# Seven large expert positions, outputs combined in quarters, and f32 one-hot picks in a two-layer mixture-of-experts kernel

## The chip, the cores and the metric

The kernel runs on one core of a Trainium2 chip, in one launch. The metric is the device time of one execution in microseconds, as the median of several. All times below are microseconds, and times of day in the trace count from the start of the span.

## The reference, cut to what matters

Two layers of a backbone. Each mixes tokens (attention and retention heads, an output projection) and then sends every token through two of 16 experts. Layer 0 does this for 512 tokens (256 latent, 256 context), layer 1 for the 256 latent ones. The expert part is:

```python
s = sigmoid(h @ w_router)
grouped = (s + b_router).reshape(-1, 4, 4)
grp = argmax(top_k(grouped, 2)[0].sum(-1))
e_idx = grp * 4 + top_k(grouped[grp], 2)[1]
gate = s[e_idx] / sum(s[e_idx])
a, u = split(x_e @ w_gu[e], 2)
y_e = (silu(a) * u) @ w_down[e]
x = x + g2 * sum_over_two_experts(gate * y_e)
```

Here h is the normalized and modulated x, w_gu[e] is 1024 x 2048, w_down[e] is 1024 x 1024, all f32, and g2 is one row of 1024 for the latent and one for the context tokens. The result must hold to f32 accuracy, so matmuls that go at full speed run on values split in a high and a low part, three products for one.

## The kernel before, in words

**Weights.** Each expert's 12 MB come as 12 pages of 1 MB (eight gate/up pages, four down pages, tile w) through one queue, SP's, into a ring of pages that x, gathered rows, outputs and constants share. The order of the stream is gate/up of expert 0, down of 0, gate/up of 1, gate/up of 2, down of 1 and so on; the last is down of expert 15. A page's transfer is issued when an earlier page has been given back.

**Positions.** The experts of a layer are run in an order that the kernel finds by counting tokens. BIG_AT names the positions that take a large expert: nine of 16 in layer 0, three in layer 1. A large position holds up to 128 rows in layer 0 (96 in layer 1): ScalarE makes the high part of each page (L190), VectorE the low part (L192), and TensorE runs three products of 128 x 512 for each logical one (L200, L201, L202; gu and dn). A small position holds up to 64 rows and multiplies the page as it is, in f32, with the rows as the stationary operand (gs at L1301, ds at L1317). The table rho says which rank by count goes to which position; position 0 is always expert 0. If an expert has more tokens than its position holds, a branch at L1387 is entered that runs every expert again in a loop, 128 rows at a time.

**Rows.** In layer 0 the rows of h are written to DRAM (HX) and an indirect DMA gathers those of an expert, which TensorE then transposes (fl, L1282). In layer 1 they stay in SBUF, in three bf16 parts (x3, L1024 to L1030), and a small expert's rows are picked by 48 one-hot bf16 matmuls (L1244; two tiles of 128 tokens, eight column blocks, three parts); for a large one by place (L1227). Index and gate of each slot come from one-hot matmuls as well (idx L1178, gates L1189, four matmuls each in layer 0).

**Routing** (route) is a chain of small VectorE steps: counts, ranks, the order, then `arranged` puts positions and gates into the order of the run; after it comes the branch. Out_proj's rows() makes h: in layer 0 two tiles on VectorE and two on ScalarE and GpSimd (L1012).

**Outputs.** An expert's rows are scattered into Y in DRAM with accumulation (L1367). After expert 13, combine reads Y back (four transfers yy in layer 0, two in layer 1, issued by GpSimd, L1535), multiplies it by g2 (L1537) and adds it to x (L1538), on VectorE. The last two experts don't go through DRAM: finish takes the down product of expert 15 in four quarters of 256 columns (L1589), spreads the rows of 14 and 15 to the tokens with one-hot matmuls (fin, L1565), multiplies by g2 (ftmp, L1575) and adds to x (L1577), where GpSimd makes one of the two adds of layer 0. A small expert's hidden rows are the product of silu(a) and u (L1306 on ScalarE, L1307 on VectorE) and are turned by TensorE (tu, L1273) ahead of its down product.

The tile framework orders the instructions of each engine when the program is built; every engine then runs them in that order.

Of the kernel before, what the change touches and what calls it, by code (L numbers as in the profile page):

```python
# [9 lines left out]
F32 = mybir.dt.float32  # L10
# [21 lines left out]
BIG_AT = [(0, 2, 4, 5, 7, 8, 10, 11, 13), (0, 4, 8)]  # L32
# [28 lines left out]
class Kernel:  # L61
# [199 lines left out]
    def late_consts(self):  # L261
# [60 lines left out]
        for l, runs in enumerate((((0, 1, 1, 15), (2, 4, 3, 0), (4, 4, 3, 4), (3, 4, 3, 8), (1, 1, 1, 12), (14, 2, 1, 13)),  # L322
                                  ((0, 1, 1, 15), (4, 2, 4, 0), (1, 3, 1, 2), (5, 3, 1, 5), (9, 7, 1, 8)))):
            for r in runs:
                i_(l, *r)
# [4 lines left out]
        self.tok = cp.tile([128, 4, 2], BF, name="tok")  # L330
        g.iota(self.tok[:, :, 0], pattern=[[128, 4]], base=-BIG, channel_multiplier=0, allow_small_or_imprecise_dtypes=True)
        g.iota(self.tok[:, :, 1], pattern=[[0, 4]], base=0, channel_multiplier=1, allow_small_or_imprecise_dtypes=True)
        self.tok2 = cp.tile([128, 4, 2], BF, name="tok2")
        v.tensor_scalar(self.tok2, self.tok, 2.0, None, op0=OP.mult)
# [568 lines left out]
    def out_proj(self, l):  # L903
# [103 lines left out]
        def rows():  # L1007
            for t in range(nt):
                b = mb[:, (t // 2) * 1024:(t // 2) * 1024 + 1024]
                if t % 2 and not l:  # L1010
                    nc.scalar.activation(xr[t], xr[t], AF.Copy, scale=rs[:, t:t + 1])
                    nc.gpsimd.tensor_tensor(xr[t], xr[t], b, op=OP.add)  # L1012
                else:
                    v.scalar_tensor_tensor(xr[t], xr[t], rs[:, t:t + 1], b, op0=OP.mult, op1=OP.add)
                nc.sync.dma_start(self.HX[l][t * 128:(t + 1) * 128, :], xr[t])
            if l:

                self.hx = [self.pgs.get("hx") for _ in range(2)]
                x3 = self.x3 = [self.hx[i // 2][1][:, (i % 2) * 1024:(i % 2) * 1024 + 1024].bitcast(BF).rearrange("p (t n) -> p t n", t=2)
                                for i in range(3)]  # L1020
                for t in range(nt):
                    nc.scalar.activation(x3[0][:, t], xr[t], AF.Copy)
                for t, rest in enumerate((ma, mb)):
                    nc.gpsimd.tensor_tensor(rest, xr[t], x3[0][:, t], op=OP.subtract)  # L1024
                    nc.scalar.activation(x3[1][:, t], rest, AF.Copy)

        def parts():
            if l:
                for t, rest in enumerate((ma, mb)):
                    v.tensor_tensor(self.x3[2][:, t], rest, self.x3[1][:, t], op=OP.subtract)  # L1030
            for i, _ in mg + xg:
                self.pgs.put(i)

        self.parts = parts

        return lg, rows


    def route(self, l, lg, rows):
# [10 lines left out]
        t1, t2 = (room[:, 320 + i * 16:320 + i * 16 + n4] for i in range(2))  # L1050
        nc.scalar.activation(s, lg[:, :nt], AF.Exp, scale=-1.0)
        warm = self.tiny("warm", [128, 1])
        nc.scalar.activation(warm, s[:, 0, 0:1], AF.Silu)
        rows()
# [24 lines left out]
        ve = g4[:, :, :, None].to_broadcast(o)  # L1079
        vo = g4[:, :, None, :].to_broadcast(o)  # L1080
        v.tensor_tensor(c1, vo, ve, op=OP.is_gt)
        v.tensor_tensor(c2, vo, ve, op=OP.is_equal)
# [15 lines left out]
        for t in range(nt):  # L1098
            nc.tensor.matmul(cnt, ones, sel[:, t], start=t == 0, stop=t == nt - 1)
        posm = self.tiny("rpm", [128, nt, 16], bufs=1)  # L1100
# [8 lines left out]
        self.indices(l, 0)  # L1109

# [6 lines left out]
        perm = sq()  # L1117
        v.tensor_tensor(perm, rank[:, None, :].to_broadcast(b16), self.rho[:, l, :, None].to_broadcast(b16), op=OP.is_equal)
        v.tensor_tensor(c3, perm, self.eid[:, None, :].to_broadcast(b16), op=OP.mult)
        od = self.tiny("rod", [128, 16], bufs=1)  # L1120
        v.tensor_reduce(od, c3, axis=AX.X, op=OP.add)
        order = self.cp.tile([128, 16], I32, name=f"order{l}")
        v.tensor_copy(order, od)

        def arranged(dst, src, e=v):
            for t in range(nt):
                m = self.sm.tile([128, 512], F32, tag="P", name="sq", bufs=3)[:, 0:256].rearrange("p (a b) -> p a b", b=16)
                e.tensor_tensor(m, perm, src[:, t, None, :].to_broadcast(b16), op=OP.mult)
                v.tensor_reduce(dst[:, t], m, axis=AX.X, op=OP.add)

        self.posm = self.tiny("rpr", [128, nt, 16], bufs=1)
        arranged(self.posm, posm)
        self.order[l] = order

# [15 lines left out]
        ve = self.ve = self.tiny("rve", [128, nt, 16, 3], BF, bufs=1)  # L1150
# [5 lines left out]
        with self.tc.issue_after(self.placed.ins):  # L1156
            self.parts()
        g = nc.gpsimd
        g.tensor_tensor(kx, s, gd[:, :, None].to_broadcast([128, nt, 16]), op=OP.mult)
        arranged(kw, kx, g)  # L1160
        for c in range(3):
            g.tensor_copy(ve[:, :, :, c], kw)
            if c < 2:
                g.tensor_tensor(kw, kw, ve[:, :, :, c], op=OP.subtract)

    def index(self, posm, S, idx, tok=None, room=None, folded=False):

        nc = self.nc
        nt = posm.shape[1]
        if room is None:  # L1170
            room = self.sm.tile([128, 512], BF, tag="oh", name="oh", bufs=2)
# [4 lines left out]
        p = self.bank("B", "idx")[:S]  # L1176
        for t in range(nt):
# [3 lines left out]
        self.placed = nc.vector.tensor_scalar(idx, p[:, 0:1], p[:, 1:2], self.halfc[:S] if folded else float(BIG), op0=OP.add, op1=OP.add)  # L1181
        return oh

    def gates(self, oh, ve, gate):

        nt, S = oh.shape[1:]
        p = self.bank("B", "gates")[:S]
        for t in range(nt):
            self.nc.tensor.matmul(p[:, 0:3], oh[:, t], ve[:, t], start=t == 0, stop=t == nt - 1)  # L1189
        self.nc.vector.tensor_reduce(gate, p[:, 0:3], axis=AX.X, op=OP.add)  # L1190

    def indices(self, l, e):
        S = self.slots(l, e)
        self.oh[e % 2] = self.index(self.posm[:, :, e], S, self.idx[:S, e:e + 1],
# [24 lines left out]
    def place(self, p, oh, b, parts=range(3)):  # L1219

        nt, S = oh.shape[1:]
        for i in parts:
            x = self.x3[i]
            for t in range(nt):
                for f in range(4):
                    c = (b * 4 + f) * 128
                    self.nc.tensor.matmul(p[:, f * S:(f + 1) * S], x[:, t, c:c + 128], oh[:, t],  # L1227
                                          start=i == t == f == 0, stop=i == 2 and t == nt - 1 and f == 3)

    def pick_up(self, l, e, b):  # L1230

        nc = self.nc
        if not self.big(l, e):
# [7 lines left out]
            for i in range(3):  # L1241
                for t in range(nt):
# [9 lines left out]
        else:  # L1252
            p = self.early[b]
            self.place(p, self.oh[0], b, (2,))
# [116 lines left out]
    def overflow(self, l):  # L1371
# [15 lines left out]
        with tc.If(n > 0):  # L1387
            for base in range(0, T - SMALL, 128):
                with tc.For_i(0, NE, 1) as e:
                    pe = self.tiny("ope", [128, nt], bufs=1)  # L1390
                    vv = self.tiny("ovv", [128, nt, 3], BF, bufs=1)
# [3 lines left out]
                    for c in range(3):  # L1395
                        nc.vector.tensor_copy(vv[:, :, c], kx)
                        nc.vector.tensor_tensor(kx, kx, vv[:, :, c], op=OP.subtract)
# [3 lines left out]
                    self.gates(self.index(pe, 128, ix, room=oh), vv, og)  # L1401
# [31 lines left out]
    def moe(self, l):  # L1433
# [24 lines left out]
        if last:  # L1458
            self.early = [self.bank("CB"[b], "pl") for b in range(2)]
            for b in range(2):  # L1460
                self.place(self.early[b], self.oh[0], b, (0, 1))
            self.overflow(l)
            room()
            pg.extend(self.hx)
            for b in range(2):
                self.pick_up(l, 0, b)
        else:
            room()
            pg.append(self.pgs.get("ex"))
            self.xg = [pg[1][1][:, b * 1024:(b + 1) * 1024] for b in range(2)]  # L1470
            nc.gpsimd.memset(pg[1][1], 0.0)
            self.expert_load(l, 0)
            self.overflow(l)
# [9 lines left out]
        def between(e):  # L1483

            def f(k):
# [5 lines left out]
                if k == 2:  # L1491
# [31 lines left out]
    def combine(self, l):  # L1523
# [12 lines left out]
        for t in range(nt):  # L1536
# [172 lines left out]
```

## Time and profile before

| | |
|---|---|
| three runs | 1628.0, 1632.47, 1633.39 (median 1632.47) |
| profiled execution | 1638.47, of which the span 1636.4 |
| TensorE, VectorE, ScalarE, GpSimd busy in the span | 1448.4, 874.8, 615.5, 161.1 |
| mean granted clock of TensorE | 0.961 of 2.4 GHz |
| moved by DMA | 515.64 MB, mean 315 GB/s |
| experts of layer 0, first gate/up product to the last add to x | 362 to 924 |
| experts of layer 1, the same | 1144 to 1633 |

A row of the trace gives its start, its length, engine, line, operation and tiles with shapes, how many alike stood together, and in brackets how long the engine had waited before it and for what. Matmul rows overlap, so a group's length is read from first to last.

### The profile page before, as it was taken

What the parts mean: (1) busy time and instruction counts of PE and PEld (TensorE: products, weight loads), DVE (VectorE), ACT (ScalarE), POOL (GpSimd) and SP (SyncE); (2) the same over time, 40 slices, a digit from 0 to 9 for tenths busy, and PEclk for the clock granted to TensorE, in tenths of its full rate; (3) what the DMA queues carried; (4) which work ended last, traced back from release to release, by engine and by line L of the source; (5) the groups of instructions that cost most, each with busy time, mean ns of one, the idle gap of its engine ahead of it and who ended that gap; (6) DMA issues with size and microseconds to landing.
All of it is one profiled execution on the core that took longest, in us unless ns stands there. A gap on an engine that the chain in (4) does not pass through costs nothing. (4 is left out here: it accounts for less than half of the span.)

```text
span 1636.4 us, 21740 instructions
## 1 busy us (share of the span) xinstructions
PE 1448.4 (89%) x7858; PEld 870.9 (53%) x7858; DVE 874.8 (53%) x1658; ACT 615.5 (38%) x922; POOL 161.1 (10%) x208
## 2 busy tenths in 40 slices
PE   5999999929999999999994799983999999988876
PEld 4767756716666567565741577762545435422213
DVE  5776576476666577575732586877525305300003
ACT  3353404225556456464630454542424304300000
POOL 2000000440010000100000400012000000000000
PEclk9999999959999999999997899996999999999998
DMA  9763679528999999999796744561899999999996
GB/s 268 288 224 132 258 267 351 180 108 340 409 405 413 391 392 353 387 390 371 292 356 262 270 134 150 189 262 40 332 419 415 418 412 419 419 414 418 417 415 225
DMA packets 115674, 515.64 MB, mean 315 GB/s; under 512 B 14145, under 2 KB 40417, under 8 KB 61922
## 3 DMA queue, kind: packets, MB, share of 16 engines
q1 hardware_dynamic: 102176, 488.67, 76.1%
q0 software_dynamic: 8016, 17.42, 3.8%
q10 hardware_dynamic: 5362, 8.03, 1.5%
q8 instruction: 65, 1.06, 0.3%
q14 instruction: 55, 0.45, 0.1%
HBM read 503.24 MB, written 17.48 MB: 318 GB/s over the span
## 5 line engine op out<-in xcount | busy, mean ns | idle before, releaser
L192 DVE TENSOR_TENSOR lo<-w,hi 128x1024 fp32r<-128x1024 f32 x342 | 417.2, 1231 | 108.8 <-ACT hi L190 36.1
L190 ACT ACTIVATE hi<-w 128x1024 fp32r<-128x1024 f32 x344 | 359.2, 1059 | 169.4 <-PE gu L202 48.4
L1301 PE MATMUL gs<-w,ex 128*64 128x512 f32 x1280 | 296.1, 600 | 24.8 <-DMA w<-in_w_gate_up_dram 24.5
L1301 PEld LDWEIGHTS gs<-w,ex 128*64 128x64 f32 x1280 | 83.2, 136 | 193.8 <-issue 130.4
L201 PE MATMUL gu<-lo,ex 128*128 128x512 f32 (+1 forms) x384 | 152.4, 397 | 0.5 <-DVE lo L192 0.5
L202 PE MATMUL gu<-hi,ex 128*128 128x512 f32 (+1 forms) x384 | 151.4, 395 | 0.0
L1317 PE MATMUL ds<-w,ex 128*64 128x512 f32 x576 | 139.7, 618 | 3.1 <-DMA w<-in_w_down_dram 3.0
L200 PE MATMUL gu<-hi,ex 128*128 128x512 f32 (+1 forms) x384 | 133.8, 405 | 7.9 <-ACT hi L190 7.7
L200 PE MATMUL px<-hi,hT 128*128 128x512 f32 (+1 forms) x304 | 114.7, 382 | 0.6 <-ACT hm L507 0.6
L201 PE MATMUL px<-lo,hT 128*128 128x512 f32 (+1 forms) x304 | 114.8, 378 | 0.0
L202 PE MATMUL px<-hi,hT 128*128 128x512 f32 (+1 forms) x304 | 114.2, 376 | 0.0
L1307 DVE TENSOR_TENSOR ex<-ex,gs 128x512 f32<-128x512 f32 x20 | 13.7, 687 | 178.9 <-PE gs L1301 178.9
L1367 POOL DMA_INDIRECT y<-ex,ridx x28 | 43.6, 1558 | 603.5 <-ACT ex L1323 357.3
L1306 ACT ACTIVATE ex<-gs 128x512 f32<-128x512 f32 x20 | 11.9, 597 | 235.0 <-PE gs L1301 235.0
L200 PEld LDWEIGHTS gu<-hi,ex 128*128 128x128 f32 (+1 forms) x384 | 70.0, 185 | 30.5 <-ACT hi L190 13.8
L201 PEld LDWEIGHTS gu<-lo,ex 128*128 128x128 f32 (+1 forms) x384 | 70.5, 184 | 22.8 <-DVE lo L192 3.9
L201 PE MATMUL dn<-lo,ex 128*128 128x512 f32 (+1 forms) x192 | 80.2, 418 | 2.1 <-DVE lo L192 1.8
L202 PEld LDWEIGHTS gu<-hi,ex 128*128 128x128 f32 (+1 forms) x384 | 70.3, 183 | 16.8
L202 PE MATMUL dn<-hi,ex 128*128 128x512 f32 (+1 forms) x192 | 77.2, 402 | 0.0
L1317 PEld LDWEIGHTS ds<-w,ex 128*64 128x64 f32 x576 | 37.6, 140 | 73.6 <-issue 56.9
L200 PE MATMUL dn<-hi,ex 128*128 128x512 f32 (+1 forms) x192 | 67.9, 411 | 1.7 <-ACT hi L190 1.6
L200 PEld LDWEIGHTS px<-hi,hT 128*128 128x128 f32 x304 | 57.0, 189 | 20.2 <-issue 5.2
(348 smaller groups left out, 1900.7 us busy)
## 6 DMA issues: line engine op xcount, KB each, us to landing
w<-in_w_gate_up_dram SPq DMA_DIRECT2D x256, 1024.0 KB, 12.0
w<-in_w_down_dram SPq DMA_DIRECT2D x128, 1024.0 KB, 11.4
w<-in_ada_w_dram SPq DMA_DIRECT2D x40, 1024.0 KB, 6.7
w<-in_w_in_dram SPq DMA_DIRECT2D x20, 1024.0 KB, 7.8
w<-in_ada_w_dram SPq DMA_DIRECT2D x16, 512.0 KB, 8.6
w<-in_w_out_dram SPq DMA_DIRECT2D x8, 1024.0 KB, 6.7
y<-zero POOLq DMA_DIRECT2D x3, 1024.0 KB, 10.7
g<-modd ACTq DMA_DIRECT2D x6, 512.0 KB, 6.3
```

What stands on the lines that cost most here:

```text
L190: nc.scalar.activation(hi, w, AF.Copy)
L192: (nc.gpsimd if after else nc.vector).tensor_tensor(lo, w, hi.bitcast(F32), op=OP.subtract)
L200: mm(o, a[0], b[0], start=first, stop=False)
L201: mm(o, a[0], b[1], start=False, stop=False)
L202: mm(o, a[1], b[0], start=False, stop=last)
L1301: nc.tensor.matmul(ps[n // 2][(n % 2) * 64:(n % 2) * 64 + 64], x[:, self.part(k)], t[:, n * 512:(n + 1) * 512], start=k == 0, stop=k == 7)
L1306: nc.scalar.activation(h, ps[0], AF.Silu)
L1307: nc.vector.tensor_tensor(h, h, ps[1], op=OP.mult)
L1317: nc.tensor.matmul(p[n * 64:n * 64 + 64], self.sx[2][:, self.part(ff)], t[:, f * 1024 + n * 512:f * 1024 + n * 512 + 512], start=ff == 0, ...
L1367: self.nc.gpsimd.indirect_dma_start(out=dst, out_offset=bass.IndirectOffsetOnAxis(ap=idx, axis=0), in_=y, in_offset=None, bounds_check=n - ...
```

## The change

1. BIG_AT of layer 0 names seven positions (0, 2, 4, 6, 8, 10, 12) where it named nine; rho follows. Positions 13, 14 and 15 are small. Layer 1 keeps its three.
2. combine only issues the reads of Y. finish does the rest by quarters: it adds Y's columns to what the one-hot matmuls gave (L1577), multiplies by g2 (L1578) and adds to x (L1580), all on VectorE. The pages of Y are kept until finish ends.
3. Layer 1 keeps x's rows in f32, without the three parts, and picks them with 16 f32 one-hot matmuls (L1257, place L1241) for the 48 in bf16.
4. Routing: out_proj hands out single rows(t), all on VectorE; the branch comes ahead of `arranged`, which goes to VectorE whole; in layer 1 the first expert's picks stand ahead of the branch; gather and its memset of layer 0's first expert come earlier.
5. Index and gate come out of one matmul per tile (L1190): the gate's columns stand beside the index's. Only expert 0's gates are still made apart (L1204).

```diff
-BIG_AT = [(0, 2, 4, 5, 7, 8, 10, 11, 13), (0, 4, 8)]
+BIG_AT = [(0, 2, 4, 6, 8, 10, 12), (0, 4, 8)]
...
+        def row(t):
+            b = mb[:, (t // 2) * 1024:(t // 2) * 1024 + 1024]
+            v.scalar_tensor_tensor(xr[t], xr[t], rs[:, t:t + 1], b, op0=OP.mult, op1=OP.add)
+            nc.sync.dma_start(self.HX[l][t * 128:(t + 1) * 128, :], xr[t])
...
+        v.tensor_tensor(kx, kw, gd[:, :, None].to_broadcast([128, nt, 16]), op=OP.mult)
+        if l:
+            self.early = [self.bank("CB"[b], "pl") for b in range(2)]
+            for b in range(2):
+                self.place(self.early[b], self.oh[0], b)
+        self.overflow(l)
+        perm = sq()
...
+        arranged(self.posm, self.posm)
+        if parts == 1:
+            arranged(ve[:, :, :, 2], kx)
...
-            nc.tensor.matmul(p[:, 0:2], oh[:, t], (self.tok2 if folded else self.tok)[:, t], start=t == 0, stop=t == nt - 1)
+            nc.tensor.matmul(p[:, 0:n], oh[:, t], ve[:, t, 0:n], start=t == 0, stop=t == nt - 1)
...
-            for i in range(3):
-                for t in range(nt):
-                    for k in range(8):
-                        nc.tensor.matmul(p[:, self.part(k)], self.x3[i][:, t, k * 128:(k + 1) * 128], oh[:, t, 0:64],
-                                         start=i == t == k == 0, stop=i == 2 and t == nt - 1 and k == 7)
+            for t in range(nt):
+                for k in range(8):
+                    nc.tensor.matmul(p[:, self.part(k)], self.xr[t][:, k * 128:(k + 1) * 128], oh[:, t, 0:64],
+                                     start=t == k == 0, stop=t == nt - 1 and k == 7)
...
-        for t in range(nt):
-            nc.vector.tensor_tensor(y[t], y[t], g2[:, (t // 2) * 1024:(t // 2) * 1024 + 1024], op=OP.mult)
-            nc.vector.tensor_tensor(self.x[t], self.x[t], y[t], op=OP.add)
-        for i, _ in yg:
-            self.pgs.put(i)
+        self.yg = yg
...
-                nc.vector.tensor_tensor(tmp, two(acc[r]), g[:, None].to_broadcast([128, 2, 256]), op=OP.mult)
-                x = two(self.xpg[r][1])[:, :, j * 256:j * 256 + 256]
-                add = (nc.gpsimd if r == 0 and pairs == 2 else nc.vector).tensor_tensor(x, x, tmp, op=OP.add)
+                nc.vector.tensor_tensor(tmp, two(acc[r]), two(self.yg[r][1])[:, :, c], op=OP.add)
+                nc.vector.tensor_tensor(tmp, tmp, g[:, None].to_broadcast([128, 2, 256]), op=OP.mult)
+                x = two(self.xpg[r][1])[:, :, c]
+                add = nc.vector.tensor_tensor(x, x, tmp, op=OP.add)
```

The order of instructions on VectorE at the end of layer 0, before (yy is what was read of Y, ex at L1307 the last small expert's hidden rows):

```order
L192 TENSOR_TENSOR lo<-w,hi 128x1024 x6
L1537 TENSOR_TENSOR yy<-yy,g_7712 128x1024
L1538 TENSOR_TENSOR xs<-xs,yy 128x1024
L1537 TENSOR_TENSOR yy<-yy,g_7712 128x1024 x2
L1538 TENSOR_TENSOR xs<-xs,yy 128x1024 x2
L1537 TENSOR_TENSOR yy<-yy,g_7712 128x1024
L1538 TENSOR_TENSOR xs<-xs,yy 128x1024
L1307 TENSOR_TENSOR ex<-ex,gs 128x512
L97 COPY ex<-tu 128x512
```

And with the change, where L1319 is what L1307 was:

```order
L192 TENSOR_TENSOR lo<-w,hi 128x1024 x8
L1319 TENSOR_TENSOR ex<-ex,gs 128x512 x2
L97 COPY ex<-tu 128x512
L1610 SCALAR_TENSOR_TENSOR ex<-ds,rgate,ex 128x512
L1610 SCALAR_TENSOR_TENSOR ex<-dn,rgate,ex 128x256
L1577 TENSOR_TENSOR ftmp<-fin,yy 128x512
L1610 SCALAR_TENSOR_TENSOR ex<-dn,rgate,ex 128x256
L1578 TENSOR_TENSOR ftmp<-ftmp,g_7190 128x512
```

The eight steps on yy no longer stand ahead of the last small expert's hidden rows; yy is first read in finish.

On TensorE at layer 1's branch (over is the number that the branch tests), with the change:

```order
L1096 MATMUL pos<-rsel,ones 128x16
L1190 MATMUL idx<-rve,oh 96x2 x2
L1241 MATMUL pl<-oh,xr 128x96 x16
L1388 TENSOR_LOAD over_9366
L1399 COMPARE_AND_BRANCH
L1401 COMPARE_AND_BRANCH
```

All 16 f32 picks of the first expert now stand ahead of the branch, where 48 in bf16 (L1227) stood before.

## Rows read from the trace of the kernel before

**Rows 1.** Stretches of 20 us: busy time (instructions), granted clock, DMA share, GB/s.
```profile
800.00:820.00 20.00, 20.00 (x94) 13.83 (x94) 13.87 (x14) 11.13 (x12) 0.00 (x0) 1.00 0.56 210
...
880.00:900.00 20.00, 7.89 (x28) 2.94 (x30) 8.79 (x8) 0.00 (x0) 0.00 (x0) 0.57 0.39 149
...
1120.00:1140.00 20.00, 4.36 (x55) 3.91 (x55) 17.16 (x55) 4.31 (x6) 7.93 (x11) 0.59 0.13 49
```

**Rows 2.** Two stretches, TensorE alone: busy (instructions), clock, DMA share, GB/s.
```profile
417.20:477.60 60.40, 60.40 (x296) 1.00 1.02 409
514.20:618.50 104.30, 98.26 (x449) 0.98 1.01 393
```

**Rows 3.** DMA of a stretch, packets and rate: 410 to 912.
```profile
DMA packets 32611, 184.70 MB, mean 368 GB/s; under 512 B 4780, under 2 KB 8868, under 8 KB 11912
```

**Rows 4.** The same of 400 to 540.
```profile
DMA packets 8684, 57.35 MB, mean 410 GB/s; under 512 B 1262, under 2 KB 1262, under 8 KB 2004
```

**Rows 5.** The same of 1180 to 1600.
```profile
DMA packets 25869, 175.03 MB, mean 417 GB/s; under 512 B 3768, under 2 KB 3768, under 8 KB 4947
```

**Rows 6.** Timeline of TensorE in layer 0: two products, then the tail.
```profile
368.40 0.39 PE L200 MATMUL gu<-hi,ex 128*128 128x512 f32 x1
368.62 0.39 PE L201 MATMUL gu<-lo,ex 128*128 128x512 f32 x1
...
872.12 1.94 PE L1301 MATMUL gs<-w,ex 128*64 128x512 f32 x8 [0.54 <-DMA w<-in_w_gate_up_dram]
892.11 1.12 PE L1273 MATMUL tu<-ident,ex 128*128 128x128 f32 x4 [18.05 <-DVE ex L1307]
...
904.19 1.95 PE L1589 MATMUL dn<-w,ex 128*64 128x256 f32 x16
...
907.88 1.95 PE L1589 MATMUL dn<-w,ex 128*64 128x256 f32 x16
```

**Rows 7.** Timeline of VectorE in the same tail.
```profile
878.62 1.23 DVE L1537 TENSOR_TENSOR yy<-yy,g 128x1024 f32<-128x1024 f32 x1 [22.92 <-DMA yy<-y]
...
891.38 0.68 DVE L1307 TENSOR_TENSOR ex<-ex,gs 128x512 f32<-128x512 f32 x1
...
910.18 0.69 DVE L1575 TENSOR_TENSOR ftmp<-fin,g 128x512 f32<-128x512 f32 x1 [3.00 <-PE fin L1565]
...
922.52 1.05 DVE L1577 TENSOR_TENSOR xs<-xs,ftmp 128x512 f32<-128x512 f32 x1
```

**Rows 8.** Waits of TensorE in layer 1, 1143 to 1632: total, times, longest.
```profile
PE gs L1301 <- DMA w<-in_w_gate_up_dram: 20.7, 29, 1.8
...
PE ds L1317 <- DMA w<-in_w_down_dram: 3.0, 6, 0.6
```

**Rows 9.** TensorE: bf16 picks of one small expert, and 32 f32 instructions of another matmul.
```profile
1208.82 1.57 PE L1244 MATMUL pl<-oh,hx 128*128 128x64 bf16 x48
...
1065.28 3.74 PE L810 MATMUL ro<-rv,am 128*128 128x128 f32 x32
```

**Rows 10.** Weight loads of that f32 matmul: min, median, max in ns.
```profile
L810 PEld LDWEIGHTS ro<-rv,am x160: 186/192/192, 206.9 to 1068.6; 128*128 128x128 f32 x160
```

**Rows 11.** Routing of layer 1 on GpSimd, VectorE and TensorE, in the timeline.
```profile
1120.51 4.20 POOL L1024 TENSOR_TENSOR mods<-xr,hx 128x1024 f32<-128x1024 f32 x2 [7.80 <-issue]
...
1117.57 2.48 DVE L1014 SCALAR_TENSOR_TENSOR xr<-xr,n2r,mods 128x1024 f32<-128x1024 f32 x2
...
1120.56 2.12 DVE L1057 TENSOR_TENSOR room<-room,brt 128x32 f32<-128x32 f32 x1
...
1142.20 0.29 PE L1189 MATMUL gates<-rve,oh 128*96 128x3 bf16 x2 [7.11 <-PEq L1387]
```

**Rows 12.** Routing of layer 0 on VectorE and GpSimd.
```profile
333.77 4.56 DVE L1014 SCALAR_TENSOR_TENSOR xr<-xr,n2r,mods 128x1024 f32<-128x1024 f32 x2
...
334.47 6.06 POOL L1012 TENSOR_TENSOR xr<-xr,mods 128x1024 f32<-128x1024 f32 x2 [1.96 <-ACT xr L1011]
```

**Rows 13.** Tail of layer 1 on TensorE.
```profile
1604.52 1.11 PE L1273 MATMUL tu<-ident,ex 128*128 128x128 f32 x4 [3.80 <-DVE ex L1307]
```

More of the change, by code (lines that the diff above doesn't have):

```diff
@@ L321, in late_consts @@
                                              allow_small_or_imprecise_dtypes=True)
[L322 removed]
+        for l, runs in enumerate((((0, 1, 1, 15), (2, 6, 2, 0), (1, 7, 2, 6), (14, 2, 1, 13)),
                                   ((0, 1, 1, 15), (4, 2, 4, 0), (1, 3, 1, 2), (5, 3, 1, 5), (9, 7, 1, 8)))):
@@ L1005, in out_proj, with route @@
             v.scalar_tensor_tensor(lg[:, t], lg[:, t], rs[:, t:t + 1], self.c0[l][:, t // 2], op0=OP.mult, op1=OP.add)
-        def rows():
-            for t in range(nt):
[L1009 to L1020, printed above, removed]
-                for t in range(nt):
[L1022 to L1025, printed above, removed]
+        def row(t):
+            b = mb[:, (t // 2) * 1024:(t // 2) * 1024 + 1024]
+            v.scalar_tensor_tensor(xr[t], xr[t], rs[:, t:t + 1], b, op0=OP.mult, op1=OP.add)
+            nc.sync.dma_start(self.HX[l][t * 128:(t + 1) * 128, :], xr[t])
         def parts():
[L1028 to L1031, printed above, removed]
+            for i, _ in mg + xg * (1 - l):
                 self.pgs.put(i)
+        self.rows, self.xr = xg, xr
         self.parts = parts
-        return lg, rows
-    def route(self, l, lg, rows):
+        return lg, row
+    def route(self, l, lg, row):
         nc = self.nc
@@ L1050, in route @@
         t1, t2 = (room[:, 320 + i * 16:320 + i * 16 + n4] for i in range(2))
+        if l == 0:
+            self.xgp = self.pgs.get("ex")
+            nc.gpsimd.memset(self.xgp[1], 0.0)
         nc.scalar.activation(s, lg[:, :nt], AF.Exp, scale=-1.0)
         warm = self.tiny("warm", [128, 1])
-        nc.scalar.activation(warm, s[:, 0, 0:1], AF.Silu)
-        rows()
+        nc.scalar.activation(warm, lg[:, 0, 0:1], AF.Silu)
+        parts = 1 if l == DEPTH - 1 else 3
+        ve = self.ve = self.tiny("rve", [128, nt, 16, 2 + parts], F32 if parts == 1 else BF, bufs=1)
+        for c in range(2):
+            nc.gpsimd.tensor_tensor(ve[:, :, :, c], self.tok[:, 0:nt, c, None].to_broadcast([128, nt, 16]),
+                                    self.rowsof[:, l, None, :].to_broadcast([128, nt, 16]), op=OP.mult)
+        row(0)
         v.tensor_scalar(s, s, 1.0, None, op0=OP.add)
@@ L1099, in route @@
             nc.tensor.matmul(cnt, ones, sel[:, t], start=t == 0, stop=t == nt - 1)
+        for t in range(1, 3 if l == 0 else 2):
+            row(t)
         posm = self.tiny("rpm", [128, nt, 16], bufs=1)
@@ L1109, in route @@
         self.indices(l, 0)
+        if l == 0:
+            row(3)
+            self.xg = [self.xgp[1][:, b * 1024:(b + 1) * 1024] for b in range(2)]
+            self.expert_load(l, 0)
         b16 = [128, 16, 16]
@@ L1116, in route @@
         v.tensor_reduce(rank, c3, axis=AX.X, op=OP.add)
[L1117 to L1133, printed above, removed]
         self.posx = posm
@@ L1155, in route, with arranged, index @@
         v.reciprocal(gd, gd)
[L1156 to L1166, printed above, removed]
+        v.tensor_tensor(kx, kw, gd[:, :, None].to_broadcast([128, nt, 16]), op=OP.mult)
[5 more added lines that the diff above has]
+        perm = sq()
+        v.tensor_tensor(perm, rank[:, None, :].to_broadcast(b16), self.rho[:, l, :, None].to_broadcast(b16), op=OP.is_equal)
+        v.tensor_tensor(c3, perm, self.eid[:, None, :].to_broadcast(b16), op=OP.mult)
+        od = self.tiny("rod", [128, 16], bufs=1)
+        v.tensor_reduce(od, c3, axis=AX.X, op=OP.add)
+        order = self.cp.tile([128, 16], I32, name=f"order{l}")
+        v.tensor_copy(order, od)
+        self.order[l] = order
+        def arranged(dst, src):
+            m = self.hip.tile([128, 1024], F32, tag="hl", name="pm", bufs=5)[:, 0:nt * 256].rearrange("p (t a b) -> p t a b", a=16, b=16)
+            o = [128, nt, 16, 16]
+            v.tensor_tensor(m, perm[:, None].to_broadcast(o), src[:, :, None, :].to_broadcast(o), op=OP.mult)
+            v.tensor_reduce(dst, m, axis=AX.X, op=OP.add)
+        self.posm = self.tiny("rpr", [128, nt, 16], bufs=1)
+        v.tensor_tensor(self.posm, posm, cap[:, None, :].to_broadcast([128, nt, 16]), op=OP.add)
+        arranged(self.posm, self.posm)
+        if parts == 1:
+            arranged(ve[:, :, :, 2], kx)
+        else:
+            arranged(kw, kx)
+            for c in range(3):
+                v.tensor_copy(ve[:, :, :, 2 + c], kw)
+                if c < 2:
+                    v.tensor_tensor(kw, kw, ve[:, :, :, 2 + c], op=OP.subtract)
+        self.parts()
+    def index(self, posm, S, idx, ve, gate=None, tok=None, room=None, folded=False):
         nc = self.nc
@@ L1217, in expert_load, with place @@
             self.gather(l, self.xg[e % 2][:, 0:512], self.idx[:, e:e + 1], True)
-    def place(self, p, oh, b, parts=range(3)):
+    def place(self, p, oh, b):
         nt, S = oh.shape[1:]
[L1222 to L1228, printed above, removed]
+        for t in range(nt):
+            for f in range(4):
+                c = (b * 4 + f) * 128
+                self.nc.tensor.matmul(p[:, f * S:(f + 1) * S], self.xr[t][:, c:c + 128], oh[:, t],
+                                      start=t == f == 0, stop=t == nt - 1 and f == 3)
     def pick_up(self, l, e, b):
@@ L1458, in moe @@
         if last:
[L1459 to L1462, printed above, removed]
             room()
-            pg.extend(self.hx)
+            pg.extend(self.rows)
             for b in range(2):
@@ L1468, in moe @@
             room()
[L1469 to L1473, printed above, removed]
+            pg.append(self.xgp)
             for b in range(2):
@@ L1490, in f @@
                         self.turn(self.h, self.sx[2], True)
-                if k == 2:
+                if k == 2 and not e:
                     self.gates(self.oh[e % 2], self.ve[:, :, e], self.gate[:self.slots(l, e), e:e + 1])
@@ L1598, in finish @@
         rest(*done)
-        for i in (self.g2[0], ti):
+        for i in (self.g2[0], ti, *(i for i, _ in self.yg)):
             self.pgs.put(i)
@@ L1672, in run @@
         K.mixers(l)
-        lg, rows = K.out_proj(l)
-        K.route(l, lg, rows)
+        lg, row = K.out_proj(l)
+        K.route(l, lg, row)
         K.moe(l)
```

47 lines of the change are left out of this document (27 added, 20 removed).

## The prediction

> **What bounds the kernel now.** I read the stretches of 20 us first, because the two layers have different limits. In layer 0's experts (362 to 924) the share of the DMA is high but not whole: it drops to 0.56 at 800 to 820 and to 0.39 at 880 to 900, and in the second of these TensorE is busy for 7.89 of 20 us at a granted clock of 0.57, so mostly at the lower of its two levels, 1.2 GHz [rows 1]. In the first TensorE is busy throughout, so pages were not given back fast enough; the second is a stall. Then two longer stretches, which compare the mix of positions: where one large and one small expert alternate they take 60.4 together, and where two large stand beside one small, the three take 104.3 and TensorE is no longer gapless [rows 2]. Then the rate of the transfers: layer 0 averages 368 GB/s from 410 to 912 [rows 3], had 410 in its early, alternating part [rows 4], and layer 1 runs at 417 for 420 us on end [rows 5]. So layer 1 is bound by its weights, and layer 0 by its engines, somewhat below the stream. Last the timeline of the tail: TensorE finishes the last small expert's gate/up at 874, then waits 18.05 for VectorE's product of its hidden rows [rows 6]. That product itself takes 0.68; VectorE could not begin it before 891.38, because the eight steps on the outputs read back from DRAM stand ahead of it, and the first of them waited 22.92 for its data [rows 7].
>
> **The change, part by part.** All durations are of the profiled execution, 1638.47 with a span of 1636.4; it stands 6.0 above the median of the runs, so I subtract from it and then take off the same 6.0.
>
> *Two large positions become small.* A large expert has 96 + 48 products 0.22 to 0.23 apart, 33 us of TensorE; a small one has 12 pages of eight instructions at 1.94, 23.3 [rows 6]. That is 9.5 saved per position, 19 for two: the low end, as it counts TensorE alone. From the stretches, a further large expert costs 104.3 - 60.4 = 43.9, so a small one 16.5, and two exchanges would give 55 [rows 2]: the high end, since it also counts the waits for splits where two large ones follow each other, which no longer happens. TensorE was still busy 98.26 of the 104.3, so the value lies near the low end: **-22**. ScalarE's and VectorE's splits of 24 pages go as well; neither bounds the new pattern, which the gapless stretch of 417 to 477 shows.
>
> *The stall in the tail.* The order shown with the change has the hidden rows' product directly behind the splits. Of 18.05 only the product's own 0.7 stays: **-17**. The wait for Y does not vanish by itself. Its reader is now the first step of finish, which stood at 910.18 [rows 7], 31.6 after the first transfer was there; the read hangs on expert 13's scatter and moves up with it. I cost it at nothing. If that cover goes, it is up to 12, what lay between the first step's start and the hidden rows' product.
>
> *The ceiling of these two.* From 410 to 912 the DMA moved 184.70 MB [rows 3]. At 410 GB/s that takes 450.5, so the stream would end at 860, 51 earlier; at 417, 59 earlier; at the 393 of the stretch with two large ones, 470, 32 earlier. The new pattern is that of the stretch with 409, so 39 fits under the ceiling, with some 12 to spare.
>
> *Index and gate in one matmul.* Fifteen groups like the 0.29 one of two matmuls [rows 11] go; at most 4 in layer 0, partly beside waits: **-2**. In layer 1 it lies under the DMA: 0.
>
> *Finish of layer 0.* Each quarter had three steps on VectorE and one on GpSimd, and now has six on VectorE of 0.69 each, 4.1 where TensorE takes 907.88 - 904.19 = 3.7 per quarter [rows 6, 7]. VectorE so becomes the bound by 0.4 each, and behind the last quarter stand all six steps instead of about three: **+4** (0 to +6). The two pages of Y are held until then; the next weights wanted are the projection's of layer 1, 13 us behind the last add, so 0.
>
> *Routing of layer 0.* Before, two tiles of rows took VectorE 4.56, because GpSimd's 6.06 ran beside them [rows 12]. Four tiles on VectorE alone cost 5.0, if two take the 2.48 which they take in layer 1 [rows 11]. `arranged`, now behind the branch, leaves the path to the branch and joins the path behind it. Taken as 0, between -3 and +5.
>
> *Routing of layer 1.* GpSimd's 4.20 of subtraction goes, beside which two tiny VectorE steps took some 2 us each, the first 2.12 [rows 11]; `arranged` goes behind the branch. Against this, 16 f32 picks stand ahead of it: 3.74 at the full clock [rows 9], up to 7.5 at half of it; 0.59 was granted there, so mostly the lower level [rows 1]. The experts start **-5** earlier (-8 to +1), and the first page of weights as well.
>
> *f32 picks in layer 1.* Forty-eight bf16 matmuls took 1.57. The trace has no f32 pick; the nearest row is a f32 matmul with the same 128 x 128 stationary operand, of which 32 instructions (two for each of 16 products) took 3.74 [rows 9]. So +2.2 per expert, and 13 small ones and two large, +32 on TensorE. The other end: if the loads, 0.192 each [rows 10], don't overlap, 6.1 per expert and +68. I take the first, since that row already holds such loads. The cover is 23.7 of TensorE's waits for weights in this layer [rows 8]; **+8** are left, and if there were none, +32. The rule that speaks against this step is in the Trainium skill, FP8 and Floating Point Precision, TensorE Precision Notes: true f32 goes through the array in four passes. Three bf16 products would so become four passes, an estimate of 2.1 instead of 3.74, and layer 1 would keep the whole of its earlier start. The row is the dearer of the two, and I go by the row.
>
> *Tail of layer 1.* The same wait, 3.80 [rows 13], becomes 0.7, and one step of 0.69 is added behind the last quarter: **-2**.
>
> Sum: layer 0 -22 - 17 - 2 + 4 = -37; layer 1 -5 + 8 - 2 = +1; together -36. From 1638.47 this is 1602.5, and less 6.0, **1596**.
>
> **The rivals.** *The stream can't go faster (0.20).* The DMA's share stood at 1.01 at 393 GB/s too [rows 2]; if this means that it was full, only its holes can be filled: 0.44 of 20 and 0.61 of 20 [rows 1], 21. Then -21 + 4 + 1 = -16: 1616. Against it stands that the same mix of weights and gathers ran at 410 earlier [rows 4]. *The whole ceiling (0.12).* The exchange is worth what the stretches say, the stream ends 51 earlier, and layer 1 keeps its early start of 5: -51 + 4 - 5 = -52: 1580. *f32 picks at their loads' pace (0.05).* +68 less 24 of cover, less 5 and 2, is +37 and eats the whole gain: 1633, no change. *The branch is taken (0.03).* This one ends slower. With seven large positions the eighth largest count of layer 0, not counting expert 0, must fit 64 rows; counted from the inputs by the reference it is exactly 64. One token more, by a near tie decided the other way in the kernel's arithmetic, and the loop runs 16 experts four times, 12 MB each: 805 MB, at 410 GB/s [rows 4] 1964, so about 3560. From the 65th token on it decides; below, it costs nothing. For it speaks only that there is no slack.
>
> **How the numbers follow.** The forecast has 0.60. Range 1576 to 1620: it holds the forecast with the bounds of its terms, the whole ceiling, and most of the case in which only the holes are filled. A measurement of this kernel can tell about 0.3% (5 us) from no change. Faster by more: the forecast and the first two rivals, 0.92, less 0.01 for bounds that fall together. Within: 0.05. Slower: 0.04.
>
> **What would show it.** Right: no wait above 1 at the hidden rows' turn in either tail; layer 0's last add near 887 in place of 922.52 [rows 7]; 400 GB/s or more from 410 to the end of layer 0's weights; a pick of 16 products near 3.7; TensorE's waits for weights in layer 1 near nothing while its end comes as much earlier as layer 0's. The forecast is wrong if the rate in layer 0 stays under 380 without a hole, if the first step of finish waits for Y, or if layer 1's experts take over 10 more than the 489 from 1144 to 1633.

## The result, and the profile after

The changed kernel takes 1613.39 as a median of four runs (1607.81 to 1615.39), the one before 1632.93: a ratio of 0.988, 95% interval 0.9846 to 0.9913, or 19.5 less. 1596 was forecast, in a range of 1576 to 1620. The profiled execution took 1607.81, the fastest of the four, at a granted clock of 0.968, where the profiled one of before, 1638.47, stood above its median, at 0.961; so the two traces differ by 30.7, more than the medians do. I use the traces to see where time went, and medians to price it.

The page of the changed kernel, the span and the busy times:

```profile
span 1606.0 us, 20671 instructions
...
PE 1451.1 (90%) x7434; PEld 872.1 (54%) x7434; DVE 799.9 (50%) x1604; ACT 562.4 (35%) x864; POOL 139.5 (9%) x195
```

TensorE is busy as long as before, in a span that is 30 shorter: what the exchange took off in layer 0 (498 to 469 between the first gate/up product and expert 15's down product), the f32 picks added in layer 1 (438 to 471 over its experts).

Stretches of layer 0, TensorE alone (us, busy, granted clock, DMA share, GB/s), to be held against [rows 2]:

```profile
416.60:537.90 121.30, 119.46 (x557) 1.00 1.02 409
537.90:664.90 127.00, 121.15 (x545) 0.99 1.02 412
664.90:799.80 134.90, 123.18 (x539) 0.97 0.96 381
799.80:865.00 65.20, 48.75 (x210) 0.97 1.01 395
```

Each of the first three is two pairs of a large and a small expert. They take 121, 127 and 135: the 60.4 per pair of [rows 2] holds at first, then the stream sets the pace at 410 GB/s, and then it falls to 381; why it falls is not shown. DMA of 405 to 870, against [rows 3]:

```profile
DMA packets 32147, 185.73 MB, mean 399 GB/s; under 512 B 4564, under 2 KB 8336, under 8 KB 11199
```

The tail of layer 0 on TensorE, against [rows 6]:

```profile
848.02 1.94 PE L1313 MATMUL gs<-w,ex 128*64 128x512 f32 x8 [1.83 <-DMA w<-in_w_gate_up_dram]
850.82 0.66 PE L1285 MATMUL tu<-ident,ex 128*128 128x128 f32 x4 [0.86 <-DVE ex L1319]
...
855.56 1.94 PE L1329 MATMUL ds<-w,ex 128*64 128x512 f32 x8 [1.84 <-DMA w<-in_w_down_dram]
...
865.05 1.95 PE L1592 MATMUL dn<-w,ex 128*64 128x256 f32 x16
```

The wait of 18.05 is 0.86, and the last two small experts now wait page by page for their weights. The down product of expert 15 begins at 865.05 instead of 904.19. VectorE in the same tail, against [rows 7]:

```profile
871.04 0.69 DVE L1577 TENSOR_TENSOR ftmp<-fin,yy 128x512 f32<-128x512 f32 x1 [3.00 <-PE fin L1566]
...
877.29 1.28 DVE L1578 TENSOR_TENSOR ftmp<-ftmp,g 128x512 f32<-128x512 f32 x2
...
881.28 4.08 DVE L1578 TENSOR_TENSOR ftmp<-ftmp,g 128x512 f32<-128x512 f32 x2
...
888.99 1.37 DVE L1580 TENSOR_TENSOR xs<-xs,ftmp 128x512 f32<-128x512 f32 x2
```

The first step of finish waits for TensorE, not for Y. But finish lasts from 865.05 to 890.4, 25.3, where it took 19.4. (The last row holds two adds; the second starts at 889.6.) One pair of multiplications took 4.08 in place of 1.28. On GpSimd there ran, at that time:

```profile
882.20 2.62 POOL L192 TENSOR_TENSOR lo<-w,hi 128x1024 fp32r<-128x1024 f32 x1 [0.15 <-PE fin L1566]
```

In layer 1, TensorE's waits from 1099 to 1603 (total, times, longest), against [rows 8] (hi at L190 is ScalarE's high part of the first page):

```profile
PE gu L200 <- ACT hi L190: 6.9, 2, 5.8
...
PE ds L1329 <- DMA w<-in_w_down_dram: 4.3, 3, 1.9
...
PE gs L1313 <- DMA w<-in_w_gate_up_dram: 1.1, 2, 0.6
```

And one small expert's f32 picks, with the groups of picks and of index matmuls in the whole program (busy, mean ns), against [rows 9]:

```profile
1141.81 3.79 PE L1257 MATMUL pl<-oh,xr 128*128 128x64 f32 x32
```
```profile
L1257 PE MATMUL pl<-oh,xr 128*128 128x64 f32 x416 | 52.9, 283 | 8.3 <-ACT ex L93 6.7 <-DVE ex L97 1.6
L1190 PE MATMUL idx<-rve,oh 128*128 128x3 f32 x52 | 7.6, 251 | 0.0
```

Waits for weights are 5.4 where they were 23.7: TensorE is layer 1's bound now. The experts of layer 1 take 498.8 from the first gate/up product to the end of the last down product, where they took 486.0. To the end of layer 1's last add it is 502.6 (1099.9 to 1602.5) where it was 489.0.

TensorE over layer 1's experts (us, busy, granted clock, DMA share, GB/s): the change; the change with nine large positions, whose layer 1 is the same program; the change with bf16 picks. The last two are runs of the next section.

```profile
1099.90:1598.70 498.80, 470.88 (x2360) 0.98 0.97 387
```
```profile
1119.20:1626.00 506.80, 478.18 (x2360) 0.97 0.96 381
```
```profile
1104.30:1589.60 485.30, 436.18 (x2568) 1.00 0.98 397
```

The first two have the same 2360 instructions, and the one with the lower clock is busy 7.3 longer. With f32 picks the clock falls in the middle of the layer. One such place in the changed kernel, with the picks ahead of it:

```profile
1271.58 2.12 PE L1257 MATMUL pl<-oh,xr 128*128 128x64 f32 x16 [0.69 <-ACT ex L93]
```
```profile
1274.00:1278.00 4.00, 4.00 (x20) 0.50 1.01 422
```

### The profile page after: what moved, and what is told of

It reads as the page before. It is cut to its first block, busy times and chain, and to the rows that moved or that the text cites. A ratio compares the mean times of both kernels' runs of the same rounds, so it can differ in the third digit from the quotient of the medians.

```text
span 1606.0 us, 20671 instructions
## 1 busy us (share of the span) xinstructions
PE 1451.1 (90%) x7434; PEld 872.1 (54%) x7434; DVE 799.9 (50%) x1604; ACT 562.4 (35%) x864; POOL 139.5 (9%) x195
## 5 line engine op out<-in xcount | busy, mean ns | idle before, releaser
L192 DVE TENSOR_TENSOR lo<-w,hi 128x1024 fp32r<-128x1024 f32 x294 | 359.1, 1231 | 100.3 <-ACT hi L190 27.2
L190 ACT ACTIVATE hi<-w 128x1024 fp32r<-128x1024 f32 x296 | 309.7, 1059 | 142.5 <-PE gu L202 47.3
L1313 PE MATMUL gs<-w,ex 128*64 128x512 f32 x1408 | 320.2, 601 | 17.8 <-DMA w<-in_w_gate_up_dram 17.5
L1313 PEld LDWEIGHTS gs<-w,ex 128*64 128x64 f32 x1408 | 95.5, 137 | 206.4 <-issue 162.7
L1319 DVE TENSOR_TENSOR ex<-ex,gs 128x512 f32<-128x512 f32 x22 | 15.1, 688 | 261.6 <-PE gs L1313 261.6
L201 PE MATMUL gu<-lo,ex 128*128 128x512 f32 (+1 forms) x320 | 129.1, 403 | 1.2 <-DVE lo L192 1.0
L202 PE MATMUL gu<-hi,ex 128*128 128x512 f32 (+1 forms) x320 | 127.9, 400 | 0.0
L200 PE MATMUL gu<-hi,ex 128*128 128x512 f32 (+1 forms) x320 | 112.9, 407 | 11.3 <-ACT hi L190 9.7
L200 PEld LDWEIGHTS gu<-hi,ex 128*128 128x128 f32 (+1 forms) x320 | 58.4, 185 | 30.4 <-ACT hi L190 14.0
L202 PEld LDWEIGHTS gu<-hi,ex 128*128 128x128 f32 (+1 forms) x320 | 59.1, 185 | 15.4
L201 PE MATMUL dn<-lo,ex 128*128 128x512 f32 (+1 forms) x160 | 66.1, 413 | 1.4 <-DVE lo L192 1.2
L202 PE MATMUL dn<-hi,ex 128*128 128x512 f32 (+1 forms) x160 | 64.5, 403 | 0.0
L201 PEld LDWEIGHTS px<-lo,hT 128*128 128x128 f32 x304 | 57.3, 188 | 12.5 <-issue 2.0
```

The source lines that it names most:

```text
L190: nc.scalar.activation(hi, w, AF.Copy)
L192: (nc.gpsimd if after else nc.vector).tensor_tensor(lo, w, hi.bitcast(F32), op=OP.subtract)
L200: mm(o, a[0], b[0], start=first, stop=False)
L201: mm(o, a[0], b[1], start=False, stop=False)
L202: mm(o, a[1], b[0], start=False, stop=last)
L1313: nc.tensor.matmul(ps[n // 2][(n % 2) * 64:(n % 2) * 64 + 64], x[:, self.part(k)], t[:, n * 512:(n + 1) * 512], start=k == 0, stop=k == 7)
```

## The experiments

Theory A was that layer 0's edits are worth their full 37 to 39, and that layer 1 gives part of it back to the f32 picks. Theory B was that the stream limits layer 0, so that each edit there gives only a part. Places in the traces of all kernels (start of expert 15's down product, start of layer 0's last add to x, first gate/up product of layer 1, length of layer 1's experts), with the medians. Each trace is of one execution, which need not be the median one:

| kernel | median | down of 15 | last add | layer 1 begins | its experts |
|---|---|---|---|---|---|
| before | 1632.9 | 904.2 | 922.5 | 1143.8 | 486.0 |
| the change | 1613.4 | 865.1 | 889.6 | 1099.9 | 498.8 |
| seven large | 1601.4 | 867.9 | 886.2 | 1107.6 | 483.4 |
| quarters | 1621.4 | 887.0 | 911.5 | 1128.9 | 481.7 |
| seven, quarters | 1597.6 | 860.8 | 885.3 | 1103.1 | 482.8 |
| change, bf16 picks | 1597.2 | 863.6 | 888.2 | 1104.3 | 485.3 |
| the same, late outputs | 1595.7 | 862.7 | 881.1 | 1100.3 | 485.2 |
| change, nine large | 1631.1 | 883.1 | 907.6 | 1119.2 | 506.8 |
| change, f32 twice | 1650.2 | 865.7 | 890.2 | 1101.2 | 541.9 |
| change, bf16 twice | 1601.6 | 864.2 | 888.7 | 1104.8 | 487.5 |
| seven, late outputs | 1592.5 | 862.6 | 880.9 | 1101.6 | 481.8 |

**Seven large positions alone**, in the kernel before:

```diff
-BIG_AT = [(0, 2, 4, 5, 7, 8, 10, 11, 13), (0, 4, 8)]
+BIG_AT = [(0, 2, 4, 6, 8, 10, 12), (0, 4, 8)]
```

> The kernel before with seven large positions in layer 0 and nothing else. Theory A (layer 0's edits are worth their full 37 to 39, and layer 1 gives some of it back to the f32 picks): two exchanges free about 22 of TensorE, the stall in the tail stays near 18, so about 1611 against 1633. Theory B (the stream limits layer 0, so each of its edits gives only a part): the stream's holes are filled only in part, about 1622.

Measured 1601.41, ratio 0.9807 (0.9791 to 0.9824), 31.7 less: more than the whole change, and 10 more than A gave. Neither theory's number was met (A 1611, B 1622). TensorE from the first gate/up product of layer 0 to expert 15's down product, before and in this run:

```profile
362.60:904.20 541.60, 498.16 (x2262) 0.96 0.94 366
```
```profile
361.40:867.90 506.50, 465.87 (x2151) 0.98 0.98 391
```

Of the 35.1 by which this stretch is shorter, 32.3 are TensorE's own busy time and 2.8 are waits. The sum of the waits hides larger moves: those for splits fell from 11.6 to 5.3 and the stall by 7.7, while those for weights rose from 3.8 to 13.4.

TensorE at its tail of layer 0:

```profile
843.68 1.94 PE L1301 MATMUL gs<-w,ex 128*64 128x512 f32 x8 [1.82 <-DMA w<-in_w_gate_up_dram]
855.94 1.11 PE L1273 MATMUL tu<-ident,ex 128*128 128x128 f32 x4 [10.33 <-DVE ex L1307]
```

The stall is still there, but 10.33 long: the last small expert now ends later against the reads of Y, since it waits for its own weights. That part of the stall is time which the stream needs anyway shows with the quarters added, below.

**Quarters alone**, in the kernel before (combine only issues the reads; finish as in the change):

```diff
-            nc.vector.tensor_tensor(y[t], y[t], g2[:, (t // 2) * 1024:(t // 2) * 1024 + 1024], op=OP.mult)
-            nc.vector.tensor_tensor(self.x[t], self.x[t], y[t], op=OP.add)
...
+                nc.vector.tensor_tensor(tmp, two(acc[r]), two(self.yg[r][1])[:, :, c], op=OP.add)
```

> The kernel before with the outputs combined by quarters in the finish and nothing else. Theory A: the 18 of stall and 3 of layer 1's go, the longer finish costs 4, so about 1617 against 1633; the wait of the hidden rows' turn falls below 1 in both layers. Theory B: the down pages of expert 15 land no earlier than before, so the stall turns into a wait for weights and the gain is 5 or less, 1628.

Measured 1621.42, ratio 0.9928 (0.9902 to 0.9955), 11.7 less, between the two theories (1617 and 1628). TensorE in its tail:

```profile
870.89 0.66 PE L1273 MATMUL tu<-ident,ex 128*128 128x128 f32 x4 [0.86 <-DVE ex L1307]
871.48 1.94 PE L1317 MATMUL ds<-w,ex 128*64 128x512 f32 x8
875.46 3.05 PE L1317 MATMUL ds<-w,ex 128*64 128x512 f32 x8 [2.04 <-DMA w<-in_w_down_dram]
```

All 17.2 of the stall go up to the down product of 15 (904.2 to 887.0), though expert 14's down pages are now waited for a little; 6.2 are lost again between there and the last add, in the longer finish. In layer 1 the longest wait at the hidden rows' turn fell from 3.8 to 0.9, as A said.

**Both**, by the two diffs above:

> The kernel before with seven large positions and the quarters, without the f32 picks, the reordered routing and the merged gates. Theory A: layer 0 gives 35 to 37, layer 1 its 2 of tail, so 1594 to 1597, faster than the whole change (1613). Theory B: about 1612, as the whole change.

Measured 1597.62, ratio 0.9785 (0.9768 to 0.9802), 35.5 less. This is A's price for layer 0 (1594 to 1597), and 15.8 better than the whole change. TensorE's waits for weights in its layer 1 stand near those of [rows 8]:

```profile
PE gs L1301 <- DMA w<-in_w_gate_up_dram: 19.2, 28, 1.8
...
PE ds L1317 <- DMA w<-in_w_down_dram: 4.3, 8, 0.6
```

The two do not add up: 31.7 and 11.7 alone, 35.5 together. With seven, the quarters take only 3.8 more, at the edge of what these runs can tell: 10.33 of stall, not 18.05, is left to take, 7.1 of it go up to expert 15's down product (waits for down pages rose from 0.5 to 4.7), and the longer finish gives 6.2 back. In the traces the rest of the gain lies in layer 1, 3.5 from layer 0's last add to the end.

**The change with bf16 picks.** The three parts are made behind the second tile's row, and rows are picked from them by bf16 matmuls as before; of the first expert's picks those from two parts stand ahead of the branch, the third behind it (cut):

```diff
-        parts = 1 if l == DEPTH - 1 else 3
+        parts = 3
...
+        if l:
+            self.heads()
```

> The whole change, but layer 1 picks its rows from three bf16 parts as before (the parts are made behind the row of the second tile; index and gates in bf16). Theory A: TensorE loses 29 of f32 picks in layer 1 and is bound by the weights again, with 4 more for the parts ahead of the branch, so some 10 to 14 faster than the whole change, 1600 to 1603. Theory B: layer 1 is bound by the weights either way, so no gain, 1613 to 1617.

Measured 1597.18, ratio 0.9788 (0.9756 to 0.9819): 16.2 faster than the change, more than the 10 to 14 of A. B falls, which had no gain here. TensorE waits for weights again, 25.2 in all, as A said. Against the run with seven and quarters it differs by the reordered routing and the merged gates alone, and these come to 0.4, no difference that this shows. The routing is not quite that of the change, since the parts are made in it: in the traces layer 1's first product comes 216.1 behind layer 0's last add, and 210.3 in the change.

**The change with nine large positions**, undoing part 1 alone:

```diff
-BIG_AT = [(0, 2, 4, 6, 8, 10, 12), (0, 4, 8)]
+BIG_AT = [(0, 2, 4, 5, 7, 8, 10, 11, 13), (0, 4, 8)]
```

> The whole change with the nine large positions of before. Theory A (parts add up: quarters 12, routing 0, f32 picks 16 lost, the exchange the rest): 1636 to 1638, no faster than before. Theory B (the f32 picks only fill time that layer 0's slower end left): 1620 to 1625.

Measured 1631.07 (ten runs, 1622.98 to 1637.56), ratio 0.9981 (0.9959 to 1.0003): no faster than before, and 5 to 7 under the sum expected. Without the exchange the other parts cancel each other. With it they cost 12: seven positions alone gave 31.7, the whole change 19.5.

**The picks made twice**, in the change (f32) and in the change with bf16 picks. The second round writes the same values again; nothing is left out. For f32 (for bf16 the loop over the three parts is doubled in the same way):

```diff
-            for t in range(nt):
+            for t in [*range(nt)] * 2:
```

> The whole change with each f32 pick of the 13 small experts of layer 1 made twice (the second writes the same values again): 13 times 3.79 = 49 more of TensorE. Theory A (TensorE is the bound of layer 1 now, 5 of waits for weights left): 44 to 49 slower, 1657 to 1662. Theory B (the weights are): under 25 slower.

> The change with bf16 picks, each of the 13 made twice: 13 times 1.57 = 20 more of TensorE, where 25 of waits for weights stand. Theory A with full cover: under 3 slower than 1597. If the cover is only 13 of the 29 of the f32 picks, as the difference of the two kernels suggests: 5 to 8 slower, 1602 to 1605.

f32 twice: 1650.15, 36.8 slower than the change by medians. In the traces layer 1's experts grew by 43.1, and 44.4 lie between the two profiled executions. The traces meet A (44 to 49); the medians lie between A and B. bf16 twice: 1601.62, 4.4 slower for 20.4 of added work, 2.6 in the traces; it was to be under 3 with full cover and 5 to 8 with part of it. TensorE's picks and waits for weights with f32 twice:

```profile
1145.79 7.36 PE L1257 MATMUL pl<-oh,xr 128*128 128x64 f32 x64
```
```profile
PE ds L1329 <- DMA w<-in_w_down_dram: 3.5, 3, 1.5
...
PE gs L1313 <- DMA w<-in_w_gate_up_dram: 0.8, 2, 0.5
```

And with bf16 twice:

```profile
PE gs L1332 <- DMA w<-in_w_gate_up_dram: 9.1, 11, 1.8
```

So TensorE hides 16 (by the medians) to 18 (by the traces) of the first 20 that are added to it, and of the 49 on top of the f32 picks only 5 (by the traces) to 12 (by the medians). The waits for weights are the cover, and with the f32 picks it is nearly used up.

**Outputs behind the last rows.** In place of the quarters, the whole-row steps of before, tied by an ordering dependency to stand behind the last small expert's hidden rows; first in the change with bf16 picks, then in the kernel before with seven large positions and nothing else:

```diff
+            with self.tc.issue_after(self.hmul.ins):
+                nc.vector.tensor_tensor(z, z, g2[:, (t // 2) * 1024:(t // 2) * 1024 + 1024], op=OP.mult)
+                nc.vector.tensor_tensor(self.x[t], self.x[t], z, op=OP.add)
```

> The whole change with bf16 picks (the kernel of the run before) and, in place of the quarters, the old whole-row steps on Y, tied to stand behind the last small expert's hidden rows; GpSimd makes one add of each quarter again. VectorE was idle for 12.3 there and the eight steps take 9.8. Theory A: layer 0's finish falls from 25 back to some 20, so 1592 against 1597. Rival: the last read of Y lands later than the hidden rows, the copies that wait behind it hold up the down product, and nothing is gained or 3 are lost, 1597 to 1600.

> The kernel before with two edits: seven large positions, and the whole-row steps on Y tied behind the last small expert's hidden rows (no quarters, no f32 picks, no reordered routing, no merged gates). Theory A (seven and the stall are all that pays; the finish keeps its 19 instead of 25): as the run with late outputs and all other edits, or 2 to 4 under seven with quarters, 1593 to 1596. Rival (the reordered routing pays too): 4 or more slower than that run's 1595.7, so 1600 or above.

The first: 1595.66, ratio 0.9782 (0.9751 to 0.9814), 1.5 less than with quarters where 5 were expected; the traces differ by 4.9, but the runs do not separate the two kernels. The second: 1592.47 over six runs, ratio 0.9767 (0.9743 to 0.9792) against 1630.45 of its own runs of before: 38.0 less, near A's 1593 to 1596. It is the lowest median of all, though not clear of the three kernels at 1596 to 1598, and some 18 (by the ratios) to 21 (by the medians) faster than the change. VectorE of the second in the tail:

```profile
847.12 0.69 DVE L1307 TENSOR_TENSOR ex<-ex,gs 128x512 f32<-128x512 f32 x1 [29.53 <-PE gs L1301]
847.72 2.35 DVE L1583 TENSOR_TENSOR yy<-yy,g 128x1024 f32<-128x1024 f32 x2
...
855.24 2.35 DVE L1584 TENSOR_TENSOR xs<-xs,yy 128x1024 f32<-128x1024 f32 x2
860.60 0.69 DVE L97 COPY ex<-tu 128x512 f32<-128x512 f32 x1 [3.01 <-PE ds L1317]
...
880.91 1.05 DVE L1573 TENSOR_TENSOR xs<-xs,ftmp 128x512 f32<-128x512 f32 x1
```

The eight steps fill the time in which VectorE waited for the down product, end before it does, and finish takes its 19 again (862.6 to 882).

## Why the prediction was right or wrong, point by point

**The verdict and its cause** were right: faster, because two large positions became small and the stall went. The time lies in the range, 17 above the forecast and nearer to the rival's 1616. By medians, along the chain of runs: exchange -31.7, quarters -3.8, routing and gates -0.4, f32 picks +16.2. Being a chain, they sum to the whole, 19.5 but for the noise of the runs of before, and that they do proves nothing. Forecast were -37 for layer 0, -5 for layer 1's routing, +8 for the picks, -2 for layer 1's tail. Of the signs that were named, the hidden rows' turn, the last add (889.6 for 887) and the pick (3.79) came as said, and the rate of 400 GB/s was missed by one. One sign of being wrong came true: layer 1's experts take 13.6 more than their 489, where 10 was the limit.

**The exchange, -22, was mis-sized; its sum with the stall was not.** Down to expert 15's down product, seven positions alone give 36.3 in the traces. The forecast took a value near its low end, 19, because TensorE was busy 98.26 of 104.3. That reading was wrong: by the busy times of the same two rows a large expert costs 98.26 - 60.40 = 37.9 and a small one 22.5, so two exchanges 31 [rows 2], and 32.3 of busy time went. The 33 for a large one counts its products at their closest spacing, without the transposes and the low clock among them: weighting the busy time in steps of 2 by the granted clock, 13.3 were lost at the lower level before and 7.7 with seven, an estimate from the two traces. The stall, -17, measured 17.2 alone and 7.1 behind the exchange. Together they came to 43.4 in that run and 39.1 in the change, where 22 + 17 + 2 = 41 were forecast. The ceiling of 51 was not reached: the stream ran at 410 to 665 and then slower. That the sum fits is luck: one term was too small, by the busy time above, and the other too large, because behind the exchange the last experts wait for their weights where the stall had been.

**The finish, +4**, was 5.9. The mechanism was right, six steps per quarter on VectorE. What I missed is that GpSimd had its own work there: 2.8 of the 5.9 are the one pair of multiplications that took 4.08. The Trainium skill, SBUF — State Buffer, section SBUF: two separate sides, says that a VectorE operation with two SBUF inputs and a GpSimd operation that reads SBUF shut each other out for a whole instruction. The trace agrees in this place, with 4.08 beside 2.62, and so do the two runs with quarters, with 4.07 and 4.09; I had used the same effect in the routing of layer 0 and not looked for it here.

**The wait for Y** was costed at nothing, and it was nothing: finish's first step waited 3.00 for TensorE.

**Routing.** In layer 0, 0 was forecast. The first expert began 6.2 earlier (362.6 to 356.4) and its gate/up took 31.9 instead of 25.9, so nothing stayed. In layer 1 the first product came 210.3 behind layer 0's last add, not 221.3, although it waited 5.8 for the first split of weights; the first expert's gate/up then took 29.5 instead of 24.3, so that about 6 stayed, near the 5 forecast. By the medians of the two runs with bf16 picks that differ in routing and gates alone, nothing came of it.

**The f32 picks are the step that failed.** Their own price was right: 3.74 forecast from a row of another matmul, 3.79 measured, so 2.2 per expert. I forecast +8 after cover; the medians say +16, the traces 9.1. Two small things were off: I counted all 23.7 of waits as cover, but 5.4 stayed as waits, and index and gate became f32 too, 7.6 busy where the bf16 ones of before took 4.9. The larger one is the clock, which the sum left at full speed. In each of the three traces with f32 picks (the change, nine large positions, f32 twice) TensorE's clock falls to 0.50, the lower of its two levels, three or four times among layer 1's experts; each of these ten places lies within a group of f32 picks or right behind it, and ahead of the group TensorE had waited 0.7 to 1.3. In the traces with bf16 picks there is none or one. Weighted in the same way, 9.7 are lost at the lower level in the change, 17.3 with nine large positions and 1.9 with bf16 picks, an estimate from these traces. Without that the experts would take 489, 489.5 and 483, so of the 13.5 between the first and the last (498.8 against 485.3) some 8 are the clock and some 6 work that found no cover. That the picks are what lets the clock fall is argued from where it falls; no run was made for it. By the Trainium skill's four passes (FP8 and Floating Point Precision, TensorE Precision Notes) the picks would have been 2.1 each, an estimate; the trace differs, 3.79, so here the neighbouring row was the better guide.

**The basis.** I assumed that the changed kernel's executions stand to their median as the profiled one of before did to its own, 6.0 above. For the profiled execution 1602.5 was forecast and 1607.81 came, 5.3 more; but it was the fastest of its kernel, 5.6 under the median. So of the 17 by which the forecast missed, 12 are this assumption. The clock goes with it: 1607.81 had 0.968 and the slowest of the change, 1615.39, had 0.965; with nine large positions 1622.98 had 0.970 and 1637.56 had 0.961; with bf16 picks 1595.24 had 0.975 and 1603.96 had 0.965. Kernels with and without f32 picks spread in this way, by 2 to 15. Why one execution gets more of the clock than another is open.

**The rivals.** That the stream can't go faster gave 1616, close to what was measured, but for another reason: with bf16 picks and the same layer 0 the kernel takes 1597. The case of f32 picks at the pace of their loads, 6.1 each, did not come. The branch was not entered: 64 tokens fit.

## What to carry to other kernels

Two gains that end at the same limit are not to be added: find how far the stream, or the next engine, lets the end move, and give the sum of both that limit. What an expert costs its engine is better read from the busy time of whole stretches than from a count of its main instructions: the count missed some 5 of 38. An edit that adds work to an engine is free only up to the waits that it can really fill: measure them by doubling the work, and look at the granted clock beside it. Where a late transfer holds up an urgent step behind it in an engine's order, first try to put the urgent step ahead; that alone, with the exchange, beat the whole change by 18 to 21.

## What had not been expected of the hardware

Sixteen f32 products with a 128 x 128 stationary operand and 64 columns took 3.79, just as those with 128 columns had taken 3.74 [rows 9]: the columns did not matter between these two. Against 48 bf16 ones in 1.57 one f32 product cost 7.2 times one in bf16 (0.237 to 0.033). The start of layer 0's experts in the changed kernel, TensorE alone (us, busy, granted clock, DMA share, GB/s):

```profile
356.00:366.00 10.00, 5.95 (x21) 0.50 0.24 81
366.00:376.00 10.00, 10.00 (x39) 0.86 0.88 367
```

TensorE had been idle at the branch, and the clock granted behind it was 0.50, the lower of its two levels, 1.2 GHz, for 10. In the kernel before, the first 10 of the first gate/up were gapless, at 0.73. The earlier branch bought time at half speed, with gaps: of the 6.2 gained nothing was left at the end of the first gate/up.
